# Weight pieces split three ahead, a larger VectorE account and re-spaced gather units in a PEER block on one Trainium2 core

## Chip, core and metric

One core of a Trainium2 chip runs the whole program in one launch. The metric is the device time of that launch in microseconds (us). TensorE (PE) multiplies, VectorE (DVE) and GpSimd (POOL) do elementwise work, ScalarE (ACT) copies and evaluates functions, SyncE (SP) issues transfers. SP, ACT and POOL each work their instructions off in the order in which they stand, and so do PE and DVE.

## What is computed

A decoder block on 512 tokens of width 2048, all in float32: a norm, an input projection, spatial gating and windowed attention, an output projection, and then a mixer that looks experts up by product keys. The mixer is where the time goes:

```python
q = (xf @ w_query).reshape(T, PEER_HEADS, 2, D_QUERY // 2)
s1 = einsum('thd,kd->thk', q[:, :, 0], sub_keys[0])      # 128 keys each
s2 = einsum('thd,kd->thk', q[:, :, 1], sub_keys[1])
v1, i1 = top_k(s1, 16); v2, i2 = top_k(s2, 16)
top_v, flat = top_k(v1[..., :, None] + v2[..., None, :], 16)   # of 256
experts = e1 * 128 + e2                                  # of 16384
gates = softmax(top_v)
u = take(expert_down, experts); a = gelu(einsum('cd,chkd->chk', x, u))
vt = take(expert_up, experts);  out = einsum('chk,chkd->cd', gates * a, vt)
```

The result is x + out, with a last norm. Each token uses 8 x 16 = 128 of the 16384 experts.

## The kernel before

The tokens are divided. For 352 of them (`TD`) the experts are computed densely: every token meets every expert, in 128 blocks of 128 experts, and a gate table that is zero where an expert was not chosen picks the right ones. For the other 160 the chosen rows are gathered from memory.

Dense work. A float32 product is made of three fast matmuls (`mm3`, L164): the weight is split into a rounded part `whi` and a rest `wlo`, the activations likewise. `down(b)` (L1015) makes block b of scores from two weight pieces of 128 x 1024, 48 matmuls of 352 columns. `up(c)` (L1042) takes eight blocks of gated scores through 16 pieces in four quarters q: the first half of a quarter uses two pieces one after the other, the second half two pieces together, 384 matmuls in all. Each of the four column groups m of a quarter is added into `accT` by VectorE at its end (L1092). The order is 88 `down`s, then ten `up`s, then one `down` and an `up`, and then eight (at the end seven) `down`s and an `up` in turn, up to `up(15)`. `make_ga` (L988) multiplies a block of scores by the gate table and splits it on ACT and DVE.

Weight pieces. `Stream` (L117) loads a piece by SP into one of four `wraw` buffers, copies it to `whi` on ACT (L143) and subtracts to `wlo` on DVE or POOL (L145), four buffers each. `get(ahead)` (L150) hands out piece p and has the pieces up to p + ahead split first; ahead is 2 unless a caller says otherwise.

Gathered work runs beside that in "units" (`unit`, L712): POOL issues an indirect transfer of 128 rows of 1024 (L706), and DVE multiplies it into sums with `half_row` (L720, in the down half) or adds it weighted (L732, in the up half). There are 512 units for the first 128 tokens and 128 for the last 32, whose 128 experts lie in four parts of 32 across the partitions. Gather buffers: four `row`, and, once the `late` pool is open (after `down(82)`), four `more`.

The planner. `Pace` (L47) decides while the program is written, at each `mm3`, what VectorE is given next. It keeps an account `vector`: `step` adds 0.98 ns for each ns of matmul, every piece of work is charged to it, and while it is above zero it hands out steps of key selection (`hot`), gate-table steps (`paced`, mostly "quads": four DVE operations L860 that build one-hot rows, then eight small matmuls L873), or a unit, if `gap` ns have passed since the last. `use_pool` (L60) sends a split to DVE when the account is above zero or POOL's own account is below it, and charges 1250; else to POOL, and charges 500. `spread` (L1190) sets `gap` once, at `down(82)`.

The end. `up(15)` also turns finished quarters back into rows (`rows_out`, L1139: 12 transposes into two `dn` buffers, DVE adds, ACT squares, a multiply), finishes the first 128 gathered tokens (`finish_first`, L1153) and the last 32 (`finish_last`, L1166: eight DVE adds of 32 rows fold the four parts), each with `last_norm` (L1119).

## Time and profile before

| | |
|---|---|
| median of three runs | 3058.1 us (3056.44 to 3060.74) |
| the profiled execution, and its span | 3053.1 us, 3051.4 us |
| busy share of the span: PE, weight loads, DVE, ACT, POOL | 94%, 89%, 74%, 38%, 48% |
| moved from and to memory | 779.91 MB, mean 256 GB/s |

The page's time slices and the view of busy time by stage show where each engine is full; the groups of instructions by line, taken in one stage, show what one operation costs there and what ended the idle time before it; the timeline shows single instructions. A mean of a group can hide two prices, and then only the timeline tells them apart. The stages are: key selection and query projection up to 784 us, `down(0)` to `down(79)` up to 1510, the change of pools and `down(80)` to `down(87)` up to 1593, `up(0)` to `up(9)` up to 2288, the alternation up to 2929, and `up(15)` with the end.

### The profile page before, as it was taken

How to read it: one execution, taken by the hardware profiler on the slowest of the kernel's cores; microseconds unless marked ns; L12 is line 12 of the kernel's file. 1: busy time of each engine (PE TensorE's matmuls, PEld its weight loads, DVE VectorE, ACT ScalarE, POOL GpSimd, SP SyncE). 2: the span in 40 equal slices, each digit the busy share in tenths (PEclk: the TensorE clock that was granted, in tenths of full speed). 3: DMA queues.
4: the chain of work that ended last, by engine and by line, in shares of the span. 5: the costliest groups of instructions: out<-in, count | busy, mean ns of one | idle time of the engine just before them, and what ended most of it. 6: DMA issues, size and time to landing. Idle time of an engine off the chain costs nothing. (4 is left out here: it accounts for less than half of the span.)

```text
span 3051.4 us, 44502 instructions
## 1 busy us (share of the span) xinstructions
PE 2867.4 (94%) x16925; PEld 2727.1 (89%) x16925; DVE 2260.2 (74%) x3359; ACT 1152.7 (38%) x1932; POOL 1474.2 (48%) x998
## 2 busy tenths in 40 slices
PE   7999999999999899999989999999999999999976
PEld 6888878799999899999988999998999999999975
DVE  3125642469947999999957888887788889778865
ACT  3244432222333456767824222322232323323223
POOL 2132100123578667777645666666665444344432
PEclk9999999999999999999999999999999999999987
DMA  5221242422379678978798999999989999899983
GB/s 191 86 83 56 76 162 90 146 90 87 122 260 343 215 264 293 317 261 316 264 333 323 357 347 342 337 334 329 353 330 347 334 334 360 315 332 335 347 306 104
DMA packets 265190, 779.91 MB, mean 256 GB/s; under 512 B 25488, under 2 KB 94416, under 8 KB 259408
## 3 DMA queue, kind: packets, MB, share of 16 engines
q1 hardware_dynamic: 151952, 382.75, 36.7%
q0 software_dynamic: 92160, 335.59, 29.0%
q10 hardware_dynamic: 20864, 58.74, 5.0%
q8 instruction: 133, 2.18, 0.3%
q14 instruction: 81, 0.66, 0.1%
HBM read 726.20 MB, written 50.77 MB: 255 GB/s over the span
## 5 line engine op out<-in xcount | busy, mean ns | idle before, releaser
L145 POOL TENSOR_TENSOR wlo<-wraw,whi 128x1024 fp32r<-128x1024 f32 x284 | 701.0, 2477 | 849.1 <-ACT whi L143 813.3
L143 ACT CAST whi<-wraw 128x1024 fp32r<-128x1024 f32 x628 | 641.2, 1048 | 679.3 <-PE up L167 326.8
L168 PE MATMUL up<-gah,wlo 128*128 128x352 f32 x2048 | 673.9, 329 | 47.2 <-POOL wlo L145 44.0
L166 PE MATMUL up<-gah,whi 128*128 128x352 f32 x2048 | 675.2, 330 | 19.9 <-DVE accT L1092 19.2
L145 DVE TENSOR_TENSOR wlo<-wraw,whi 128x1024 fp32r<-128x1024 f32 x344 | 462.1, 1350 | 305.5 <-ACT whi L143 303.8
L166 PE MATMUL dn<-h2d,whi 128*128 128x352 f32 x2048 | 667.3, 326 | 15.2 <-ACT whi L143 15.2
L168 PE MATMUL dn<-h2d,wlo 128*128 128x352 f32 x2048 | 669.7, 327 | 5.8 <-POOL wlo L145 3.6
L167 PE MATMUL up<-gal,whi 128*128 128x352 f32 x2048 | 668.9, 327 | 0.0
L167 PE MATMUL dn<-h2d,whi 128*128 128x352 f32 x2048 | 667.0, 326 | 0.0
L168 PEld LDWEIGHTS up<-gah,wlo 128*128 128x128 f32 x2048 | 394.0, 192 | 56.9 <-POOL wlo L145 53.2
L166 PEld LDWEIGHTS up<-gah,whi 128*128 128x128 f32 x2048 | 394.4, 193 | 27.5 <-DVE accT L1092 18.0
L166 PEld LDWEIGHTS dn<-h2d,whi 128*128 128x128 f32 x2048 | 390.8, 191 | 16.1 <-ACT whi L143 16.1
L168 PEld LDWEIGHTS dn<-h2d,wlo 128*128 128x128 f32 x2048 | 389.5, 190 | 10.3 <-POOL wlo L145 6.9
L167 PEld LDWEIGHTS up<-gal,whi 128*128 128x128 f32 x2048 | 394.7, 193 | 0.0
L167 PEld LDWEIGHTS dn<-h2d,whi 128*128 128x128 f32 x2048 | 389.7, 190 | 0.0
L720 DVE SCALAR_TENSOR_TENSOR row<-row,half_row 128x1024 f32<-128x1024 f32 x236 | 282.6, 1211 | 70.0 <-DMA row<-in_down_rows,idx 55.7
L860 DVE SCALAR_TENSOR_TENSOR p<-iota,eT,gT 128x256 fp32r<-128x256 f32 x352 | 317.0, 959 | 1.9 <-PE tr L873 1.9
L706 POOL DMA_INDIRECT row<-in_down_rows,idx x236 | 249.3, 1056 | 140.5 <-DVE row L720 88.7
L706 POOL DMA_INDIRECT more<-in_up_rows,idx x160 | 184.4, 1152 | 162.0 <-DVE half_row L732 136.3
L706 POOL DMA_INDIRECT row<-in_up_rows,idx x160 | 182.9, 1143 | 145.3 <-DVE half_row L732 115.7
L732 DVE SCALAR_TENSOR_TENSOR half_row<-more,wgt,half_row 128x1024 f32<-128x1024 f32 x160 | 205.1, 1282 | 1.5 <-DMA more<-in_up_rows,idx 0.3
L732 DVE SCALAR_TENSOR_TENSOR half_row<-row,wgt,half_row 128x1024 f32<-128x1024 f32 x156 | 200.0, 1282 | 1.7 <-DMA row<-in_up_rows,idx 0.3
(201 smaller groups left out, 3755.7 us busy)
## 6 DMA issues: line engine op xcount, KB each, us to landing
wraw<-in_down SPq DMA_DIRECT2D x256, 512.0 KB, 5.6
wraw<-in_up SPq DMA_DIRECT2D x256, 512.0 KB, 7.0
wraw<-in_win SPq DMA_DIRECT2D x52, 512.0 KB, 3.8
g_dram<-stage ACTq DMA_DIRECT2D x22, 1024.0 KB, 8.2
g<-g_dram SPq DMA_DIRECT2D x32, 704.0 KB, 9.3
wraw<-in_wout SPq DMA_DIRECT2D x32, 512.0 KB, 3.7
wraw<-in_wq SPq DMA_DIRECT2D x32, 512.0 KB, 3.7
aa<-a_dram SPq DMA_DIRECT2D x88, 176.0 KB, 9.1
```

The source lines that it names most:

```text
L143: self.nc.scalar.copy(hi, src)
L145: eng.tensor_sub(lo, src, hi.bitcast(F32))
L166: nc.tensor.matmul(ps, wh, xh, start=start, stop=False)
L167: nc.tensor.matmul(ps, wh, xl, start=False, stop=False)
L168: nc.tensor.matmul(ps, wl, xh, start=False, stop=stop)
L706: nc.gpsimd.indirect_dma_start(out=t, out_offset=None, in_=src, in_offset=bass.IndirectOffsetOnAxis(ap=idx[i][:, j, h:h + 1], axis=0))
L720: nc.vector.scalar_tensor_tensor(t, t, 1.0, half_row, op0=OP.mult, op1=OP.mult, accum_out=dots[i][:, j, h:h + 1])
L732: nc.vector.scalar_tensor_tensor(half_row, t, wgt[i][:, j:j + 1], half_row, op0=OP.mult, op1=OP.add)
L860: nc.vector.scalar_tensor_tensor(p2[:, j], iota[:, None, :].to_broadcast([P, 2, P]), t[:, 1, k:k + 1], hl[:, k, :, None].to_broadcast([P, ...
```

## The change

- `get(3)` in `down` and in the first halves of `up`: three pieces ahead are split there, with the same four buffers.
- The account grows by 1.12 ns per ns of matmul (0.98 before), and `use_pool` keeps a split on DVE down to an account of -300.
- No unit or step is handed out while column groups 2 and 3 of a second half are written (`pace.held`).
- Units: the gap is 2300 ns up to `down(82)` (2600 before); from then on `spread(at)` sets it anew at each `up`, from the matmul time left less 110 us. The `more` buffers are three.
- In `up(15)`: `rest_of_first` runs at q = 2, not 1. The last 32 tokens are folded by a matmul with a 0/1 matrix `ones`, one 512-column step ahead of each column group of the last quarter, in place of the eight adds. The three row blocks' `last_norm`s stand behind all three blocks' adds and multiplies.
- `FULL`, `used` and the partial table end change nothing here, since 352 = 11 x 32.

```diff
-MORE_ROWS = 4
+MORE_ROWS = 3
...
-        self.gap = 2600.0
+        self.gap = 2300.0
...
     def use_pool(self):
-        if self.vector > 0.0 or self.pool < 0.0:
+        if self.vector > -300.0 or self.pool < 0.0:
...
-        self.vector = max(min(self.vector + 0.98 * ns, 3000.0), -4000.0)
+        self.vector = max(min(self.vector + 1.12 * ns, 3000.0), -4000.0)
...
     def down(b):
-            hi, lo = W.get()
+            hi, lo = W.get(3)
...
             for i in range(2):
-                w = W.get()
+                w = W.get(3)
...
-            if last and q == 1:
+            if last and q == 2:
                 rest_of_first()
-            if last and q == 2:
                 pace.drain()
-                rest_of_last = finish_last()
-            if last and q == 3:
-                rest_of_last()
+                steps_of_last.extend(finish_last())
...
             for m in range(4):
+                pace.held = m > 1
+                if last and q == 3 and steps_of_last:
+                    steps_of_last.pop(0)()
                 for j in range(4, 8):
                     multiply(m, j, w[j // 2 - 2])
...
+            pace.held = False
...
             square(b, n, y, q, nc.vector if q == 3 else nc.gpsimd)
-            if q == 3:
-                last_norm(b, n, y, o_rows[b + 1][:n])
+        if q == 3:
+            for b in range(ND):
+                n = min(P, TD - b * P)
+                last_norm(b, n, late["x"][b], o_rows[b + 1][:n])
...
-                eng = nc.sync if s % 2 else nc.scalar
-                eng.dma_start(t[:n], y_dram[1][s * n:(s + 1) * n, cols])
-                parts.append((t, cols))
-
-        def rest():
-            for t, cols in parts:
-                nc.vector.tensor_add(x[:n, cols], x[:n, cols], t[:n])
-            for q in range(4):
-                square(NB, n, x, q, nc.vector)
-            last_norm(NB, n, x, o_rows[NB - 1][P - n:])
-        return rest
+            t = pg.tile([P, D // 2], F32, name="row", bufs=4)
+            nc.sync.dma_start(t, y_dram[1][:, h * D // 2:(h + 1) * D // 2])
+            parts.append(t)
+        ones = late["fin"].tile([P, EX], F32, name="ones")
+        nc.vector.tensor_reduce(ones, ident.rearrange("p (s m) -> p m s", m=EX), axis=AX.X, op=OP.add)
+
+        def piece(q):
+            cols = slice(q * 512, (q + 1) * 512)
+            ps = ps2.tile([P, 512], F32, name="dn", bufs=2)
+            nc.tensor.matmul(ps[:n], ones, parts[q // 2][:, q % 2 * 512:(q % 2 + 1) * 512],
+                             start=True, stop=True)
+            nc.vector.tensor_add(x[:n, cols], ps[:n], x[:n, cols])
+            square(NB, n, x, q, nc.gpsimd)
+            if q == 3:
+                last_norm(NB, n, x, o_rows[NB - 1][P - n:])
+        return [lambda q=q: piece(q) for q in range(4)]
...
-        pace.gap = (left * TD * COL_NS - 45e3) / len(pace.units)
+            pace.gap = max(2000.0, (left - 110e3) / len(pace.units))
```

What the planner makes of it shows in the order of the instructions. On DVE, in the middle of the 88 `down`s, before (`p` is a quad's one-hot rows, `row` a unit, `oh` and `ef` steps of decoding the keys):

```order
L720 SCALAR_TENSOR_TENSOR row,dots_4083<-row,half_row 128x1024
L860 SCALAR_TENSOR_TENSOR p_11132<-iota,eT,gT 128x256 x4
L720 SCALAR_TENSOR_TENSOR row,dots_4083<-row,half_row 128x1024
L644 TENSOR_TENSOR oh<-dec,iota 128x1024
L649 TENSOR_TENSOR oh<-oh,keyf 128x1024
L651 TENSOR_REDUCE ef<-oh 128x64
L860 SCALAR_TENSOR_TENSOR p_11247<-iota,eT,gT 128x256 x4
L720 SCALAR_TENSOR_TENSOR row,dots_4083<-row,half_row 128x1024
L860 SCALAR_TENSOR_TENSOR p_11295<-iota,eT,gT 128x256 x4
```

and now, on DVE in the same stretch:

```order
L861 SCALAR_TENSOR_TENSOR p_9705<-iota,eT,gT 128x256 x4
L721 SCALAR_TENSOR_TENSOR row,dots_4083<-row,half_row 128x1024
L146 TENSOR_TENSOR wlo<-wraw,whi 128x1024
L721 SCALAR_TENSOR_TENSOR row,dots_4083<-row,half_row 128x1024
L861 SCALAR_TENSOR_TENSOR p_9773<-iota,eT,gT 128x256 x4
L146 TENSOR_TENSOR wlo<-wraw,whi 128x1024
L721 SCALAR_TENSOR_TENSOR row,dots_4083<-row,half_row 128x1024 x2
L861 SCALAR_TENSOR_TENSOR p_9840<-iota,eT,gT 128x256 x4
L721 SCALAR_TENSOR_TENSOR row,dots_4083<-row,half_row 128x1024 x2
```

Units come in pairs, and splits stand on DVE where there were none. On DVE in the stretch of ten `up`s, around a second half, before:

```order
L145 TENSOR_TENSOR wlo<-wraw,whi 128x1024 x2
L732 SCALAR_TENSOR_TENSOR half_row<-more,wgt_4081,half_row 128x1024
L1092 TENSOR_TENSOR accT<-up,accT 128x352
L732 SCALAR_TENSOR_TENSOR half_row<-more,wgt_4081,half_row 128x1024
L1092 TENSOR_TENSOR accT<-up,accT 128x352 x2
L732 SCALAR_TENSOR_TENSOR half_row<-more,wgt_4081,half_row 128x1024
L1092 TENSOR_TENSOR accT<-up,accT 128x352
L145 TENSOR_TENSOR wlo<-wraw,whi 128x1024
```

and now there:

```order
L146 TENSOR_TENSOR wlo<-wraw,whi 128x1024 x2
L733 SCALAR_TENSOR_TENSOR half_row<-row,wgt_4081,half_row 128x1024 x3
L146 TENSOR_TENSOR wlo<-wraw,whi 128x1024
L733 SCALAR_TENSOR_TENSOR half_row<-row,wgt_4081,half_row 128x1024
L146 TENSOR_TENSOR wlo<-wraw,whi 128x1024
L733 SCALAR_TENSOR_TENSOR half_row<-more,wgt_4081,half_row 128x1024
L1099 TENSOR_TENSOR accT<-up,accT 128x352
L733 SCALAR_TENSOR_TENSOR half_row<-more,wgt_4081,half_row 128x1024
L1099 TENSOR_TENSOR accT<-up,accT 128x352 x3
```

No unit stands any more between the last three adds of a quarter, and the split that followed the second half stands ahead of its adds. On DVE in `up(15)`, q = 1 and the start of q = 2, before (`xr` are the dense tokens' rows, `yf` the first gathered tokens):

```order
L145 TENSOR_TENSOR wlo<-wraw,whi 128x1024
L732 SCALAR_TENSOR_TENSOR half_row<-more,wgt_4082,half_row 128x1024
L1160 TENSOR_TENSOR yf<-yf,xf 128x2048
L1122 TENSOR_REDUCE sf<-ss_26853 128x1
L1128 TENSOR_SCALAR yf<-yf,rstd 128x1024
L1148 TENSOR_TENSOR xr_26854<-dn,xr_26854 128x512
L1148 TENSOR_TENSOR xr_26856<-dn,xr_26856 128x512
L1148 TENSOR_TENSOR xr_26858<-dn,xr_26858 96x512
L145 TENSOR_TENSOR wlo<-wraw,whi 128x1024 x2
```

and now:

```order
L146 TENSOR_TENSOR wlo<-wraw,whi 128x1024 x3
L1156 TENSOR_TENSOR xr_26884<-dn,xr_26884 128x512
L1156 TENSOR_TENSOR xr_26886<-dn,xr_26886 128x512
L1156 TENSOR_TENSOR xr_26888<-dn,xr_26888 96x512
L146 TENSOR_TENSOR wlo<-wraw,whi 128x1024
L1099 TENSOR_TENSOR accT<-up,accT 128x352 x4
L146 TENSOR_TENSOR wlo<-wraw,whi 128x1024 x3
L1170 TENSOR_TENSOR yf<-yf,xf 128x2048
L1130 TENSOR_REDUCE sf<-ss_26883 128x1
L1136 TENSOR_SCALAR yf<-yf,rstd 128x1024
```

The gathered tokens' steps stand a quarter later, and no unit is left in this block. Counted over the whole program, splits on DVE go from 344 to 429 and on POOL from 284 to 199; the number of units, 640, stays.

## Rows read from the trace of the kernel before

**Rows 1.** Busy time by stage: stretch, length, PE, PEld, DVE, ACT, POOL, clock, DMA.

```profile
784.00:1057.00 273.00, 257.88 (x1564) 254.27 (x1564) 208.45 (x410) 97.65 (x136) 204.62 (x116) 0.97 0.71 247
1057.00:1510.00 453.00, 445.22 (x2928) 443.56 (x2927) 445.76 (x549) 311.60 (x699) 335.69 (x192) 0.99 0.82 286
1510.00:1593.40 83.40, 72.58 (x451) 70.76 (x450) 50.50 (x79) 34.29 (x70) 36.37 (x26) 0.94 0.89 329
1593.40:2287.60 694.20, 643.96 (x3840) 630.85 (x3841) 564.79 (x717) 208.74 (x261) 429.94 (x301) 0.97 0.91 339
2287.60:2929.10 641.50, 622.43 (x3842) 618.20 (x3841) 542.71 (x619) 200.00 (x245) 288.41 (x242) 0.99 0.93 337
2929.10:3051.40 122.30, 73.81 (x434) 71.65 (x432) 69.61 (x83) 35.95 (x62) 27.24 (x28) 0.80 0.48 175
```

**Rows 2.** The same view of single blocks: eight downs, up(3), up(11).

```profile
2363.80:2425.30 61.50, 61.50 (x387) 61.50 (x386) 52.48 (x53) 21.10 (x30) 24.55 (x22) 1.00 0.90 316
1803.00:1871.50 68.50, 63.64 (x386) 62.56 (x386) 53.62 (x86) 20.15 (x25) 44.04 (x32) 0.98 0.92 342
2425.30:2488.50 63.20, 61.72 (x386) 61.14 (x386) 57.24 (x59) 18.18 (x19) 29.75 (x25) 1.00 0.98 362
```

**Rows 3.** PE by line, 1593 to 2288 us: busy, mean ns, idle before, releasers.

```profile
L168 PE MATMUL up<-gah,wlo 128*128 128x352 f32 x1280 | 423.4, 331 | 39.8 <-POOL wlo L145 39.4
L166 PE MATMUL up<-gah,whi 128*128 128x352 f32 x1280 | 423.2, 331 | 10.8 <-DVE accT L1092 10.1 <-ACT whi L143 0.4 <-ACT accT L1090 0.3
```

**Rows 4.** Waits of the whole run: total us, times, longest us.

```profile
PE up L168 <- POOL wlo L145: 44.0, 25, 3.8
```

**Rows 5.** ACT by line, 1593 to 2288 us.

```profile
L143 ACT CAST whi<-wraw 128x1024 fp32r<-128x1024 f32 x161 | 163.8, 1049 | 233.9 <-PE up L167 146.8 <-DMA wraw<-in_up 46.6 <-POOL wlo L145 38.7
```

**Rows 6.** DVE by line, 1593 to 2288 us.

```profile
L145 DVE TENSOR_TENSOR wlo<-wraw,whi 128x1024 fp32r<-128x1024 f32 x89 | 147.2, 1659 | 37.1 <-ACT whi L143 36.7
...
L1092 DVE TENSOR_TENSOR accT<-up,accT 128x352 f32<-128x352 f32 x143 | 73.2, 518 | 39.1 <-PE up L168 38.8
...
L999 DVE TENSOR_TENSOR gal<-aa,gah 128x352 fp32r<-128x352 f32 x81 | 42.5, 525 | 49.7 <-ACT gah L998 49.7
```

**Rows 7.** DVE by line, 2296 to 2812 us: splits with POOL almost without any.

```profile
L145 DVE TENSOR_TENSOR wlo<-wraw,whi 128x1024 fp32r<-128x1024 f32 x126 | 153.4, 1220 | 31.6 <-ACT whi L143 31.2 <-PE dn L168 0.4
```

**Rows 8.** DVE by line, 1057 to 1510 us.

```profile
L860 DVE SCALAR_TENSOR_TENSOR p<-iota,eT,gT 128x256 fp32r<-128x256 f32 x312 | 287.3, 979 | 1.5 <-PE tr L873 1.5
L720 DVE SCALAR_TENSOR_TENSOR row<-row,half_row 128x1024 f32<-128x1024 f32 x96 | 115.1, 1208 | 4.2 <-DMA row<-in_down_rows,idx 4.1
```

**Rows 9.** POOL by line, 1057 to 1510 us.

```profile
L145 POOL TENSOR_TENSOR wlo<-wraw,whi 128x1024 fp32r<-128x1024 f32 x96 | 240.2, 2504 | 85.2 <-ACT whi L143 84.3
```

**Rows 10.** Timeline of DVE and POOL: start, length, instruction, idle before.

```profile
1230.70 3.81 DVE L860 SCALAR_TENSOR_TENSOR p<-iota,eT,gT 128x256 fp32r<-128x256 f32 x4
...
1277.24 1.67 DVE L860 SCALAR_TENSOR_TENSOR p<-iota,eT,gT 128x256 fp32r<-128x256 f32 x4
...
1231.59 2.63 POOL L145 TENSOR_TENSOR wlo<-wraw,whi 128x1024 fp32r<-128x1024 f32 x1 [1.52 <-ACT whi L143]
```

**Rows 11.** DVE by line, 784 to 1057 us.

```profile
L720 DVE SCALAR_TENSOR_TENSOR row<-row,half_row 128x1024 f32<-128x1024 f32 x51 | 61.2, 1214 | 35.7 <-DMA row<-in_down_rows,idx 35.6
```

**Rows 12.** PE by line in up(15), 2929 us to the end.

```profile
L1145 PE MATMUL dn<-ident,accT 128*128 128x128 f32 (+1 forms) x48 | 7.8, 301 | 25.9 <-DVE xr L1148 25.6 <-DVE accT L1092 0.3
```

**Rows 13.** Timeline of DVE in up(15) and at the end.

```profile
2963.82 2.29 DVE L1160 TENSOR_TENSOR yf<-yf,xf 128x2048 f32<-128x2048 f32 x1 [7.72 <-DMA xf<-x_dram]
...
2972.84 0.75 DVE L1128 TENSOR_SCALAR yf<-yf,rstd 128x1024 f32<-128x1024 f32 x1 [3.51 <-POOL rstd L1126]
...
3004.48 4.95 DVE L1184 TENSOR_TENSOR xf<-xf,more 32x1024 f32<-32x1024 f32 x4
...
3033.47 0.75 DVE L1128 TENSOR_SCALAR xr<-xr,rstd 128x1024 f32<-128x1024 f32 x1 [0.95 <-POOL rstd L1126]
...
3041.54 0.75 DVE L1128 TENSOR_SCALAR xr<-xr,rstd 96x1024 f32<-96x1024 f32 x1 [0.94 <-POOL rstd L1126]
```

More of the change, by code (lines that the diff above doesn't have):

```diff
@@ L40 @@
 TG = 32
-NTG = TD // TG
+NTG = -(-TD // TG)
+FULL = TD // TG
 BIG = 3.0e38
 COL_NS = 0.4505
-MORE_ROWS = 4
+MORE_ROWS = 3
 class Pace:
@@ L882, in products @@
                                                           bufs=4)
+                            used = TD - b * P - 4 * n
+                            if used < TG:
+                                nc.gpsimd.memset(stage[h][:, :, used:], 0.0)
                     o = 4 * (n % 8)
@@ L1171, in finish_last, with spread @@
         for h in range(2):
[L1172 to L1195 removed]
+            t = pg.tile([P, D // 2], F32, name="row", bufs=4)
[13 more added lines that the diff above has]
+        return [lambda q=q: piece(q) for q in range(4)]
+    steps_of_last = []
+    def spread(at):
+        left = sum(48 if k == "d" else 384 for k, i in order[at:]) * TD * COL_NS
+        if pace.units:
+            pace.gap = max(2000.0, (left - 110e3) / len(pace.units))
+    for at, (kind, i) in enumerate(order):
         if kind == "u":
+            spread(at)
             up(i)
```

21 lines of the change are left out of this document (7 added, 14 removed).

## The prediction

> **What bounds the kernel now.** I read the busy time by stage first [rows 1], then single blocks [rows 2], then the groups by line in the stages that lose time, and last the timeline where a group's mean mixes two prices.
>
> PE is the engine to be kept busy. A clean block, eight `down`s with 384 matmuls, takes 61.5 us [rows 2], 0.160 us a matmul. By that rate the ten `up`s (3840 matmuls) need 614 us and take 694: 80 lost. The alternation behind them needs 615 and takes 641.5: 27 lost. `up(15)` needs 61.5 and takes 122 with the end of the program [rows 1]. The reader should see that these three stages, with the change of pools, hold the slack; and that VectorE is nearly full in most of the kernel, at 445.8 of 453 us in the second part of the `down`s.
>
> In the ten `up`s PE waits 39.4 us for a `wlo` from POOL and 10.1 us for `accT`, whose add must free the accumulator [rows 3]; the granted clock is 0.97 there, and 3% of 694 is 21 us of lower clock (1.2 instead of 2.4 GHz, after PE stood still). Together 71 of the 80. The longest wait for POOL is 3.8 us [rows 4]. A `wlo` is late because its piece is (46.6 us of ACT's idle time ahead of `whi` is a transfer of `wraw` [rows 5]), because it takes 2.4 us or more on POOL, and because gathers stand ahead of it in POOL's queue.
>
> In the quads' part of the `down`s VectorE and POOL hold each other up. Four quad operations take 1.67 us alone and 3.81 us when a POOL split of 2.63 us runs among them [rows 10], so the mean of 979 ns [rows 8] is a mixture: 78 quads at 1.67 would be 130 us, they take 287, and the other 157 us belong to 96 POOL splits [rows 9], 1.6 us each.
>
> **The change part by part.** The sum is made against the profiled execution, 3053.1 us (its span is 3051.4, 1.7 lies around it). It is 5.0 under the median, which I add at the end. The numbers of units and splits by stage are counted along the program before and after.
>
> A. `down(0)` to `down(79)`, 784 to 1510 us. 57 units are done here that stood later (147 become 204): 57 x 1.21 = 69 us more for VectorE [rows 8]. 38 splits come from POOL: 38 x 1.22 = 46 us [rows 7]. 31 of them leave the quads' part, at 1.6 us each: 50 us less. Seven key-selection steps go ahead of 784, 16 us by what the code charges for them; VectorE isn't what PE waits for there, and I charge nothing. Balance: +49 us of VectorE time. VectorE is busy 654 of 726 us and idle 72 [rows 1]; 40 of these it waits for gathered rows [rows 8, 11], and I keep that. The other 32 are spots where it was ahead, and I keep 8. So 654 + 49 + 48 = 751: **+25 us**. If a POOL split costs VectorE 2.1 us wherever it meets quads (3.81 - 1.67) and the idle time falls to 25: 654 + 33 + 25 = 712, -14. If the denser units wait more, 85 us idle: +62, which is the upper end.
>
> B. The change of pools, 83.4 us with PE busy 72.6 [rows 1]. A piece is copied ahead of the first `make_ga`s on ACT, not behind them: up to one piece's time, 24 x 0.16 = 3.8 us. **-3** (-9 to +6).
>
> C. The ten `up`s. Per block 4.1 splits leave POOL (7.2 become 3.1), 2.6 units have gone to A (23 become 20.4), 4 more splits stand on DVE. What leaves PE's path: each first-half piece is split 24 matmuls, 3.84 us, sooner, and the longest wait for POOL was 3.8; a split on DVE takes 1.22, not 2.4; no unit delays the last two adds of a quarter, so most of the 10.1 us goes. What is late next is VectorE. Before, it is busy 56.5 us a block and idle 5 more waiting for ACT in `make_ga` (49.7 in all [rows 6]): 61.5, just what PE needs. Now: splits 4 x 1.22 = +4.9; units 2.6 x 1.21 = -3.1; its splits took 1659 ns against 1220 alone [rows 6, 7], 39 us over 72 POOL splits, 0.54 each, so 4.1 x 0.54 = -2.2. Sum -0.4: as full as before. The nearest row is `up(11)`, which took 63.2 us with VectorE busy 57.2 and almost no such waits [rows 2]; `up(3)` with them took 68.5. I take 65.1 a block: **-43 us**. At 63.2 it is -62, at 67.9 (VectorE makes PE wait where POOL did) -15.
>
> D. 2288 to 2929 us. 27 us lost; here nearly all splits are on DVE already, and lead and held units act alone. Two losses come with the change from the first to the last gathered tokens, and come again elsewhere. Half: **-14** (-25 to 0).
>
> E. `up(15)` and the end. PE waits 25.9 us ahead of row transposes [rows 12], twice: at q = 1 while DVE holds at `yf` for a transfer and then for its chain over ACT and POOL, from 2956 to 2973.6, and at q = 3 behind the fold, two groups of 4.95 and the multiplies [rows 13]. The first wait goes, since row blocks no longer stand behind `yf`. The chain itself (2963.8 to 2973.6, 9.8 us [rows 13]) now stands ahead of the next row blocks at q = 2, with two pieces of lead less: I keep 8 us of it. The second wait goes; four short matmuls cost about 2 us, an estimate from the 7.8 us of 48 transposes, and the last 32 tokens' norm, now ahead of the last `accT` add, 1.5. Splits waited 2 to 3 us more, and clock after two stalls 3 us less. -25.9 + 8 + 2 + 1.5 - 6 = **-20** (-27 to -8). The last norms side by side give nothing: the blocks follow each other at 4.04 us (8.07 for two [rows 13]), of which 1.85 is a norm (0.15 + 0.95 + 0.75); DVE still does a norm's sum, waits for POOL and scales before the next, and the three parts only change places. All three output transfers now start within 4 us, which may cost 1.
>
> Sum: 25 - 3 - 43 - 14 - 20 = -55. 3053.1 - 55 = 2998; with the 5.0, **3003 us**.
>
> The Trainium skill ("Perfetto Trace Analysis", Optimizing Scalar/DVE Operations) says that where VectorE is saturated, handing work to another engine, GpSimd too, may help. This change does the opposite in A. By that rule alone the 50 us of relief would not exist. The same section warns that the two share an SBUF read port and so may gain nothing from it, and 3.81 against 1.67 us [rows 10] is on the side of the warning.
>
> **The rivals.**
> 1. VectorE's larger account is hidden in A: the stage ends at its lower bound, -14. Sum -94: 2964. For it: PE itself needs 80 x 48 x 0.16 = 614 us of the 726 there, and the quads' small matmuls. Against: VectorE is at 98% [rows 1]. Chance 0.16.
> 2. VectorE stays the bound in C, -15: the sum is -27, 3031. For it: 61.5 us of work and waits in 61.5. Against: the waits shown are for POOL. Chance 0.18.
> 3. Relief fails: POOL splits delay VectorE as much as before although they are fewer (the lock is met by what is left, and by the new DVE splits). A is then +75: sum -5, 3053. Chance 0.06. This is also what the cited rule would give.
> 4. Slower: **the gather queue in A.** Only four `row` buffers exist there, and units now come in pairs, 204 in the place of 147. Where they stood densest before, VectorE waited 35.6 us over 51 units, 0.70 each [rows 11]; in the quads' part 4.1 over 96 [rows 8]. VectorE works in order, so each such wait holds splits and quads behind it, and PE behind those. At 0.70 for all 204: 143 us in the place of 40, A is 654 + 49 + 143 + 8 - 726 = +128, and the sum +48: 3106. It decides from a mean wait of about 0.47 us a unit, where A eats up the other terms. Against: the quads' part spaced units at 4.7 us and now at some 3.6, nearer to its row than to the other. Chance 0.13.
>
> **How the numbers follow.** The forecast, 2985 to 3022, has 0.47. Rivals 1 and 2 are faster too. Within 0.2% (6 us, about what a measurement of this kernel can tell from no change) I put rival 3's middle and a little of rival 2's upper end; slower is rival 4 and the rest of rival 3. Faster 0.80, same 0.06, slower 0.14. The range leaves out most of rival 4 and the lower half of rival 1: 2964 to 3055.
>
> **What would show it.** Right: the ten `up`s near 651 us with under 15 us of PE waiting for `wlo` and clock near 1.0; the `down` stage near 751 us, VectorE still above 95% busy and quads nearer to 1.67 us; no idle time ahead of L1145's first group in `up(15)`, but one of some 8 us ahead of the second; the last three norms no shorter. Wrong: VectorE idle for rows in A by far more than 40 us (rival 4); PE in the `up`s waiting for DVE as long as it did for POOL (rival 2); a `down` stage no longer than 726 us (rival 1).

## The result and the profile after

The changed kernel takes 3037.9 us (median of 5 runs, 3034.2 to 3043.4), the kernel before, run beside it, 3060.7 (3056.4 to 3064.6). The ratio is 0.9927, with a 95% interval of 0.9911 to 0.9943: faster by 22.8 us, where 55 were forecast. The profiled execution after is 3037.9 us long with a span of 3036.2, right at its median. The profiled execution before, 3053.1, stands 7.6 us under the median of these five runs. The traces thus show 15.2 us between the two spans, and the medians 22.8.

The busy time by stage of the kernel after (stretch, length, PE, PEld, DVE, ACT, POOL, granted clock, DMA share, GB/s); the stages start at the first matmul of `down(0)`, `down(24)`, `down(80)`, `up(0)`, `down(88)` and `up(15)`, so they answer to [rows 1], except that the downs are cut at another place:

```profile
786.70:1000.60 213.90, 193.45 (x1158) 190.35 (x1157) 181.46 (x401) 67.49 (x81) 148.08 (x88) 0.96 0.75 261
1000.60:1576.00 575.40, 540.46 (x3352) 529.88 (x3353) 539.02 (x726) 352.00 (x766) 363.12 (x239) 0.96 0.85 301
1576.00:1651.60 75.60, 69.29 (x434) 68.48 (x433) 45.56 (x76) 30.02 (x58) 33.60 (x24) 0.95 0.87 321
1651.60:2305.90 654.30, 628.36 (x3842) 620.34 (x3842) 548.00 (x676) 208.47 (x261) 303.64 (x235) 0.98 0.92 341
2305.90:2931.20 625.30, 617.35 (x3842) 614.23 (x3842) 521.81 (x607) 205.84 (x250) 249.69 (x209) 1.00 0.90 326
2931.20:3036.20 105.00, 73.74 (x441) 67.98 (x439) 43.52 (x62) 34.20 (x60) 27.00 (x27) 0.88 0.46 162
```

and the same view of the kernel before for the first three and the next seven groups of eight `down`s:

```profile
784.00:977.20 193.20, 188.01 (x1154) 185.41 (x1154) 138.30 (x316) 63.71 (x76) 148.89 (x85) 0.99 0.72 251
977.20:1510.30 533.10, 515.40 (x3339) 512.72 (x3338) 516.20 (x644) 345.70 (x759) 391.42 (x223) 0.98 0.80 279
```

The reader should see that the later stages gave about what was forecast, and that the downs took most of it back. After minus before: the part ahead of the downs +2.7, the downs (A) +20.7 and +42.3, together +63; the change of pools (B) -7.5; the ten ups (C) -39.9; the alternation (D) -16.2; `up(15)` and the end (E) -17.3. In sum -15.

In the downs 3 to 9 the two engines' groups by line say what PE waits for. PE, kernel after, then before (busy, mean ns, idle before, releasers):

```profile
L874 PE MATMUL tr<-p,p 128*128 128x128 f32 x656 | 98.1, 280 | 34.9 <-DVE p L861 34.8
```

```profile
L873 PE MATMUL tr<-p,p 128*128 128x128 f32 x640 | 83.4, 271 | 12.0 <-DVE p L860 10.8 <-ACT whi L143 1.2
L842 PE MATMUL tr<-ident,ef 128*128 128x128 f32 x9 | 2.2, 317 | 5.7 <-DVE ef L651 4.8 <-DVE ef L665 1.0
```

Nearly all of PE's idle time after, 575.4 - 540.5 = 35 us, stands ahead of the quads' products, which wait for VectorE's `p`; before it was 12 and 5.7. PE is also busy longer, 540 us where nearly the same matmuls took 515. The granted clock explains about half of these 25 us: 0.96 in the mean loses 0.04 x 575 = 23 us, 0.98 before lost 0.02 x 533 = 11. Where the rest comes from is open. VectorE is what the stage waits for. Its groups in the same stretch, after:

```profile
L861 DVE SCALAR_TENSOR_TENSOR p<-iota,eT,gT 128x256 fp32r<-128x256 f32 x332 | 271.7, 877 | 0.0
L721 DVE SCALAR_TENSOR_TENSOR row<-row,half_row 128x1024 f32<-128x1024 f32 x158 | 188.1, 1212 | 30.4 <-DMA row<-in_down_rows,idx 29.0 <-ACT half_row L720 1.1
L146 DVE TENSOR_TENSOR wlo<-wraw,whi 128x1024 fp32r<-128x1024 f32 x32 | 40.6, 1269 | 4.4 <-ACT whi L144 4.4
L645 DVE TENSOR_TENSOR oh<-dec,iota 128x1024 bf16<-128x1024 f32 x8 | 19.6, 2449 | 0.0
...
L652 DVE TENSOR_REDUCE ef<-oh 128x64 f32<-128x1024 bf16 x8 | 9.8, 1220 | 0.3
```

and before:

```profile
L860 DVE SCALAR_TENSOR_TENSOR p<-iota,eT,gT 128x256 fp32r<-128x256 f32 x331 | 304.3, 977 | 1.5 <-PE tr L873 1.5
L720 DVE SCALAR_TENSOR_TENSOR row<-row,half_row 128x1024 f32<-128x1024 f32 x111 | 133.1, 1209 | 12.8 <-DMA row<-in_down_rows,idx 12.6
```

The units and the new splits bring 55 and 41 us; the quads give back 33. POOL still makes 81 splits there (112 before):

```profile
L146 POOL TENSOR_TENSOR wlo<-wraw,whi 128x1024 fp32r<-128x1024 f32 x81 | 196.9, 2431 | 49.0 <-ACT whi L144 47.8
```

In the first three groups of downs VectorE waits less for rows than before (27.3 us there):

```profile
L721 DVE SCALAR_TENSOR_TENSOR row<-row,half_row 128x1024 f32<-128x1024 f32 x46 | 54.9, 1213 | 18.3 <-DMA row<-in_down_rows,idx 13.4 <-ACT asp L1040 4.8
```

In the ten ups PE's wait for POOL's `wlo`, 39.4 us [rows 3], is gone, and its wait for `accT` has grown from 10.1 to 17.9:

```profile
L167 PE MATMUL up<-gah,whi 128*128 128x352 f32 x1280 | 418.6, 327 | 23.9 <-DVE accT L1099 17.9 <-ACT whi L144 4.8 <-ACT accT L1097 1.3
...
L169 PE MATMUL up<-gah,wlo 128*128 128x352 f32 x1280 | 415.7, 325 | 2.0 <-DVE wlo L146 1.2 <-POOL wlo L146 0.7
```

In `up(15)` 25.9 us ahead of the row transposes [rows 12] have become 11.8. By the timeline of PE, 8.18 of them are a single wait at the start of the second group, the chain of the gathered tokens:

```profile
L1153 PE MATMUL dn<-ident,accT 128*128 128x128 f32 (+1 forms) x48 | 7.4, 289 | 11.8 <-DVE xr L1156 9.2 <-DVE accT L1099 2.6
```

```profile
2980.52 1.09 PE L1153 MATMUL dn<-ident,accT 128*96 128x128 f32 x4 [8.18 <-DVE xr L1156]
```

### The profile page after: what moved, and what is told of

It reads as the page before. It is cut to its first block, busy times and chain, and to the rows that moved or that the text cites. A ratio compares the mean times of both kernels' runs of the same rounds, so it can differ in the third digit from the quotient of the medians.

```text
span 3036.2 us, 44558 instructions
## 1 busy us (share of the span) xinstructions
PE 2875.5 (95%) x16933; PEld 2729.3 (90%) x16933; DVE 2256.4 (74%) x3437; ACT 1162.6 (38%) x1932; POOL 1276.6 (42%) x917
## 4 chain that ended last, share of the span: by engine, by line
PE 60%; DVE 18%; DMA 10%; issue 5%; POOL 3%; ACT 2%; SPq 0%; ACTq 0%; POOLq 0%; DVEq 0%
PE up L167 7%; PE up L169 7%; PE up L168 7%; PE acc L167 7%; PE acc L169 7%; PE acc L168 7%; PE dn L168 5%; PE dn L167 5%; PE dn L169 5%; DVE p L861 4%; DMA wraw<-in_up 4%; DVE row L721 4%; DMA row<-in_down_rows,idx 3%; DVE wlo L146 2%; DMA row<-in_up_rows,idx 2%
## 5 line engine op out<-in xcount | busy, mean ns | idle before, releaser
L146 POOL TENSOR_TENSOR wlo<-wraw,whi 128x1024 fp32r<-128x1024 f32 x199 | 492.1, 2479 | 850.9 <-ACT whi L144 815.7
L146 DVE TENSOR_TENSOR wlo<-wraw,whi 128x1024 fp32r<-128x1024 f32 x429 | 528.1, 1242 | 294.1 <-ACT whi L144 293.9
L707 POOL DMA_INDIRECT row<-in_down_rows,idx x275 | 297.8, 1083 | 304.7 <-DVE row L721 243.3
L721 DVE SCALAR_TENSOR_TENSOR row<-row,half_row 128x1024 f32<-128x1024 f32 x275 | 328.0, 1213 | 75.1 <-DMA row<-in_down_rows,idx 60.1
L707 POOL DMA_INDIRECT row<-in_up_rows,idx x182 | 210.2, 1155 | 174.6 <-DVE half_row L733 152.2
L861 DVE SCALAR_TENSOR_TENSOR p<-iota,eT,gT 128x256 fp32r<-128x256 f32 x352 | 279.7, 854 | 0.0
L733 DVE SCALAR_TENSOR_TENSOR half_row<-row,wgt,half_row 128x1024 f32<-128x1024 f32 x181 | 232.5, 1284 | 5.2 <-DMA row<-in_up_rows,idx 2.9
L707 POOL DMA_INDIRECT more<-in_up_rows,idx x138 | 160.2, 1161 | 118.4 <-DVE half_row L733 90.0
L1005 ACT CAST gah<-aa 128x352 fp32r<-128x352 f32 x128 | 62.3, 487 | 310.7 <-DVE aa L1001 272.2
## 6 DMA issues: line engine op xcount, KB each, us to landing
g_dram<-stage ACTq DMA_DIRECT2D x22, 1024.0 KB, 10.1
```

The costliest lines, as they stand in the source:

```text
L146: eng.tensor_sub(lo, src, hi.bitcast(F32))
L707: nc.gpsimd.indirect_dma_start(out=t, out_offset=None, in_=src, in_offset=bass.IndirectOffsetOnAxis(ap=idx[i][:, j, h:h + 1], axis=0))
L721: nc.vector.scalar_tensor_tensor(t, t, 1.0, half_row, op0=OP.mult, op1=OP.mult, accum_out=dots[i][:, j, h:h + 1])
L733: nc.vector.scalar_tensor_tensor(half_row, t, wgt[i][:, j:j + 1], half_row, op0=OP.mult, op1=OP.add)
L861: nc.vector.scalar_tensor_tensor(p2[:, j], iota[:, None, :].to_broadcast([P, 2, P]), t[:, 1, k:k + 1], hl[:, k, :, None].to_broadcast([P, ...
L1005: nc.scalar.copy(hi, t)
```

## The experiments

Three groups, each on one chip beside runs of the kernel before. The times by stage in the tables are cut at the same matmuls as above.

### Lead and account, each alone

The first kernel is the one before with only the lead of three:

```
-            hi, lo = W.get()
+            hi, lo = W.get(3)
...
-                w = W.get()
+                w = W.get(3)
```

> The kernel before with three pieces ahead alone (in down and in up's first halves); account, gap and the end as before. Theory 1 (the lead of 3.84 us is what frees the ten ups, the account is what lengthens the downs): downs 0 to 79 stay at 726 us (within 6), the ten ups fall from 694 to 655 to 665, the last block stays at 122, total 30 to 40 us under the kernel before. Theory 2 (the gain in the ups comes from splits moved to VectorE and from units moved out of them): the ups stay above 680, total within 15 us of before.

Measured: 3070.6 us, ratio 1.0025 (0.9996 to 1.0055): no gain. PE in the ten ups:

```profile
L166 PE MATMUL up<-gah,whi 128*128 128x352 f32 x1280 | 426.8, 333 | 31.3 <-DVE accT L1092 26.1 <-ACT whi L143 4.5 <-issue 0.6
...
L168 PE MATMUL up<-gah,wlo 128*128 128x352 f32 x1280 | 421.9, 330 | 17.4 <-POOL wlo L145 17.2 <-DVE wlo L145 0.2
```

The earlier split does shorten the wait for POOL, from 39.4 to 17.2 us, but the wait for `accT` grows from 10.1 to 26.1, and the ups take 697 us where they took 694. One wait took the place of the other. So the second theory's marks hold, but neither theory had the downs right: both left them at 726 us, and they take 195.7 + 568.3 = 764. It is the downs 3 to 9 that grew, with a quad operation at 1089 ns beside 113 POOL splits:

```profile
980.30:1548.60 568.30, 529.45 (x3346) 520.07 (x3345) 552.91 (x648) 351.65 (x763) 385.83 (x226) 0.97 0.76 265
```

```profile
L860 DVE SCALAR_TENSOR_TENSOR p<-iota,eT,gT 128x256 fp32r<-128x256 f32 x332 | 342.2, 1089 | 0.0
```

The second kernel has only the new account:

```
-        self.gap = 2600.0
+        self.gap = 2300.0
...
-        if self.vector > 0.0 or self.pool < 0.0:
+        if self.vector > -300.0 or self.pool < 0.0:
...
-        self.vector = max(min(self.vector + 0.98 * ns, 3000.0), -4000.0)
+        self.vector = max(min(self.vector + 1.12 * ns, 3000.0), -4000.0)
```

> The kernel before with the account alone (1.12, -300, gap 2300 up to down 82); two pieces ahead, units in up spaced by one gap set at down 82. Theory 1: downs 0 to 79 lengthen from 726 to about 789 us as in the changed kernel, the ups gain 10 to 20 (POOL makes 3 splits a block, not 7), total 30 to 50 us slower than before. Theory 2: the ups fall to 655 or less and the total is within 25 us of the kernel before or under it. If two pieces ahead make PE stall more, the downs exceed 800.

Measured: 3052.1 us, ratio 0.9956 (0.9926 to 0.9985). Downs 3 to 9 and the ups:

```profile
1003.50:1582.10 578.60, 536.85 (x3352) 524.20 (x3353) 542.77 (x726) 349.03 (x766) 365.90 (x239) 0.97 0.84 299
...
1661.90:2314.80 652.90, 630.44 (x3841) 619.15 (x3840) 560.94 (x672) 209.20 (x261) 325.93 (x236) 0.98 0.91 338
```

The account alone makes the ups as short as in the changed kernel (654.3), as the second theory had it, with two pieces of lead and nothing held back, and makes the downs as long. Both the gain in C and the loss in A belong to it.

### The account in one part, and quads without POOL

The changed kernel with the account of before up to the change of pools:

```
-        self.gap = 2300.0
+        self.gap = 2600.0
+        self.rate, self.floor = 0.98, 0.0
...
             open_late()
+            pace.rate, pace.floor = 1.12, -300.0
             spread(at)
```

> The changed kernel with the account of before (0.98, 0, gap 2600) up to down 82 and its own from there. The downs then do 147 units as before, so the ups get 23 a block. Theory 1: downs 0 to 79 back to 726 us (within 8), that is 63 less than in the changed kernel; the ups give back part: 660 to 672 in the place of 654; the rest as in the changed kernel; total 40 to 55 us under the changed kernel. Rival (three pieces ahead is what lengthens the downs, by binding ACT and VectorE to PE's progress): downs stay above 770, total within 10 us of the changed kernel.

Measured: 3088.6 us, ratio 1.0077 (1.0040 to 1.0114). Neither expectation held: all downs take 763 us, between the 726 of the one and the 770 of the other, and the whole is 51 us over the changed kernel. The downs 3 to 9 still take 568 us (with the lead of three, as in the first kernel), and the ups 698. In the ups 23 units a block are left, as before the change, and only 3 to 4 splits a block are on POOL: PE hardly waits for POOL there, but long for `accT`.

```profile
PE up L168 <- DVE accT L1100: 37.6, 21, 5.2
...
PE up L170 <- POOL wlo L147: 2.6, 2, 1.7
```

So to take the splits from POOL without moving units out of the ups brought nothing here. This and the first kernel say that lead and account in the ups are not enough.

Now the suspicion in A: that POOL's splits hold up the quads. The changed kernel, with every split on VectorE while quads are pending:

```
-        if self.vector > -300.0 or self.pool < 0.0:
+        if self.vector > -300.0 or self.pool < 0.0 or 0 < len(self.paced) < 104:
```

> The changed kernel with every split on VectorE while quads are made (about downs 22 to 80), none on POOL. The account then hands out 158 units in downs 0 to 79, not 204. Lock theory (a POOL split costs VectorE 1.6 us where it meets quads, more than the 1.22 us of the split itself): a quad falls from 3.3 us on average to 1.67, VectorE's work in downs 24 to 79 from 78 to about 68 us per eight downs, PE becomes the bound: downs 0 to 79 fall from 789 to 725 to 745; ups 660 to 670; total 35 to 60 us under the changed kernel. Rival (VectorE is simply full, a split handed to it costs its 1.22 us): 80 more splits are 98 us less 46 units at 1.2, downs 0 to 79 at 810 to 840, total 20 to 60 us over the changed kernel.

Measured: 3018.7 us, ratio 0.9862 (0.9808 to 0.9917), 19 us under the changed kernel (in another group of runs), though VectorE has 81 more splits in the downs 3 to 9. Some 35 to 60 were expected. The downs, 721 us in all, went by the lock theory (725 to 745), the ups (660 to 670) did not. The downs 3 to 9, and the ups:

```profile
999.60:1505.70 506.10, 506.10 (x3343) 506.06 (x3344) 426.86 (x716) 349.35 (x759) 131.48 (x112) 0.99 0.83 293
...
1578.70:2267.80 689.10, 639.76 (x3842) 629.68 (x3841) 571.21 (x750) 209.59 (x262) 331.89 (x260) 0.97 0.92 343
```

```profile
L861 DVE SCALAR_TENSOR_TENSOR p<-iota,eT,gT 128x256 fp32r<-128x256 f32 x332 | 138.7, 480 | 0.0
```

A quad operation takes 480 ns in the mean, 877 in the changed kernel. PE is busy all of the time: 506 us is its own time there. VectorE's busy time falls from 539 to 427 us, though part of that is work that went elsewhere: the splits, charged to the account, leave 46 fewer units in this stage; the ups have 23 units a block again and take 689 us.

### Quads without POOL, and the units kept

To take the two apart, a split in the quads' part is charged at 700 instead of 1250, which gives the same number of units to each stage as the changed kernel has:

```
-        if self.vector > -300.0 or self.pool < 0.0:
-            self.vector -= 1250.0
+        quads = 0 < len(self.paced) < 104
+        if self.vector > -300.0 or self.pool < 0.0 or quads:
+            self.vector -= 700.0 if quads else 1250.0
```

> The changed kernel, with every split on VectorE while quads are pending (as in the run with quads without GpSimd), and such a split charged 700 ns to the account in place of 1250, so that the planner sets the same 156 units into the downs 3 to 9 as the changed kernel does (the earlier run had 110 there) and 20 to 21 into each up block. Theory 'lock': the downs lose their time to GpSimd splits that hold up the quads' VectorE operations, and the units as such fit beside TensorE: downs 3 to 9 take 506 to 525 us (575 in the changed kernel), quads 0.48 us each, the ten ups 650 to 660 as in the changed kernel, in all some 2965 to 2990 us. Rival 'VectorE time': 46 more units at 1.28 us add 59 us of VectorE work to the 427 us of the earlier run, and with them the downs go to 550 us or more; in all 3010 or more. Rival 'DMA in the downs': 24 MB more in the downs 3 to 9 would need 340 GB/s there; if transfers then wait, the idle time is in front of wlo and whi, and the stretch takes 530 to 550.

Measured: 2974.3 us, ratio 0.9716 (0.9666 to 0.9766): faster than both kernels. Downs 3 to 9, ups, alternation, and VectorE's groups in the first of these:

```profile
999.60:1515.60 516.00, 512.68 (x3351) 509.88 (x3352) 478.49 (x813) 351.94 (x771) 193.98 (x158) 0.99 0.92 336
...
1586.70:2241.10 654.40, 627.78 (x3842) 620.31 (x3841) 549.15 (x679) 209.32 (x262) 303.21 (x235) 0.98 0.92 341
2241.10:2864.10 623.00, 616.96 (x3842) 614.38 (x3841) 520.42 (x605) 204.36 (x248) 249.09 (x209) 1.00 0.90 326
```

```profile
L722 DVE SCALAR_TENSOR_TENSOR row<-row,half_row 128x1024 f32<-128x1024 f32 x158 | 189.4, 1214 | 20.1 <-DMA row<-in_down_rows,idx 20.1
L862 DVE SCALAR_TENSOR_TENSOR p<-iota,eT,gT 128x256 fp32r<-128x256 f32 x338 | 141.2, 479 | 0.0
L147 DVE TENSOR_TENSOR wlo<-wraw,whi 128x1024 fp32r<-128x1024 f32 x113 | 137.6, 1219 | 15.9 <-ACT whi L145 15.8
...
L653 DVE TENSOR_REDUCE ef<-oh 128x64 f32<-128x1024 bf16 x8 | 9.8, 1220 | 0.3
L646 DVE TENSOR_TENSOR oh<-dec,iota 128x1024 bf16<-128x1024 f32 x8 | 9.8, 1219 | 0.0
```

The same 158 units that are said to cost the stage 55 us now stand beside PE: 516 us instead of 575. 81 splits on POOL cost more than 81 x 1.22 = 99 us of splits on VectorE. All other stages are within 5 us of the changed kernel's, and 64 us are gained (between two groups of runs).

The same with the account of before in the first three groups of downs, once with 500 and once with 700 as the charge:

```
-        self.vector = max(min(self.vector + 1.12 * ns, 3000.0), -4000.0)
+        rate = 0.98 if len(self.paced) >= 104 else 1.12
+        self.vector = max(min(self.vector + rate * ns, 3000.0), -4000.0)
```

(with the limit of -300 set to 0 there too).

> As the run with the same units and no GpSimd splits, but the account of before (0.98 for a nanosecond, limit 0) for the first three down blocks, and a charge of 500 ns in the quads' part so that some 17 more units go there. Theory 'account at the start': the 20 us that the first three downs gained in the changed kernel (193 to 214 us) come from the larger account alone, which brings splits and units among the choices' VectorE work: the first three downs fall back to 194 to 197 us, and the whole to some 15 to 20 us less than the run it is built on, unless the extra units cost downs 3 to 9 more than 5 us. Rival 'order of the choices': the 20 us come from steps that the ahead of three moves; then the first three downs stay at 212 to 216.

> As the run with the same units and no GpSimd splits (2974 us), with the account of before for the first three down blocks and the charge of 700 ns kept. First three downs 197 to 201 us in place of 215; downs 3 to 9, into which the quads that the small account puts off now fall, with 11 GpSimd splits at their start: 520 to 535 in place of 516 (540 in the run with 500 ns, which set 17 more units there); ups 655 to 668, since some 7 units more are left. If the first stage's gain is kept by the others: 2960 to 2970 us; if work that is put off is only paid later: 2974 to 2985.

Measured: 2985.4 us, ratio 0.9755 (0.9703 to 0.9807), and 2975.7 us, ratio 0.9687 (0.9654 to 0.9720). The first three groups fall to 199.7 and 199.0 us (215.5), so 16 of the 20 us that they had grown are the account's. But the next stage takes 539.9 and 523.4 (516.0), and the alternation 630 and 633 (623). In the second kernel 16 us are gained, and the stages behind pay back 19 in sum: work that is put off is paid later. The second kernel's expectation of 520 to 535 held. The first kernel's did not: it was to be 15 to 20 us faster than the run that it is built on, with 5 us at most for the extra units, and is 11 slower.

### What bounds the ups

The kernels up to here move 338 to 343 GB/s in the ups, at a DMA share of 0.91 to 0.92. That looked like a limit, with the units' bytes as its cause. Two kernels on the base of the one before, which keep the order: half of each gather, and half of each unit's VectorE work.

```
+            c = D // 4 if "p" in late else D // 2
+            short[fetched] = c < D // 2
             nc.gpsimd.indirect_dma_start(
-                out=t, out_offset=None, in_=src,
+                out=t[:, :c], out_offset=None,
+                in_=src.rearrange("r (a c) -> (r a) c", c=c),
...
+            if short[u]:
+                x = t[:, None, :D // 4].to_broadcast([P, 2, D // 4])
+                z = half_row.rearrange("p (a c) -> p a c", a=2)
...
-                    nc.vector.scalar_tensor_tensor(half_row, t, wgt[i][:, j:j + 1], half_row,
+                    nc.vector.scalar_tensor_tensor(z, x, wgt[i][:, j:j + 1], z,
...
```

> The kernel before, from the first up block's opening on each gather fetches 2 KB for a partition in place of 4 KB (half of each row, of other places of the table), and VectorE works over 1024 elements as before by reading the half row twice. So half of the gathered values are left out of the sums. Nothing else moves in the order. Theory 'bytes': the ups run at what the DMA engines deliver, 338 to 343 GB/s in five kernels; ten ups move 235 MB, of which 60 MB are then gone, and they fall from 694 us to TensorE's 620 to 640 us, the alternation from 641 to 618 to 628, and the whole by 70 to 95 us. Rival 'VectorE time': the ups are bound by VectorE's units and splits and the waits behind them; then the ups stay at 680 to 700.

```
+            c = D // 4 if "p" in late else D // 2
...
-                nc.vector.scalar_tensor_tensor(t, t, 1.0, half_row, op0=OP.mult, op1=OP.mult,
+                nc.vector.scalar_tensor_tensor(t[:, :c], t[:, :c], 1.0, half_row[:, :c], op0=OP.mult, op1=OP.mult,
...
-                    nc.vector.scalar_tensor_tensor(half_row, t, wgt[i][:, j:j + 1], half_row,
+                    nc.vector.scalar_tensor_tensor(half_row[:, :c], t[:, :c], wgt[i][:, j:j + 1], half_row[:, :c],
```

> The kernel before, from the first up block's opening on each unit's VectorE operation works over 512 of the 1024 gathered elements, and the gathers stay whole. So half of the gathered values are left out of the sums. VectorE is relieved of some 23 times 0.55 us in an up block, 12 to 14 us of 56. Theory 'bytes': the ups stay within 8 us of 694, the whole within 15 us of before. Rival 'VectorE time': the ups fall by 60 us or more, as they would if VectorE's work set their end.

Measured, the ups with half the gathers, then with half the VectorE work:

```profile
1602.70:2292.10 689.40, 639.12 (x3841) 626.53 (x3842) 564.51 (x717) 206.73 (x261) 438.08 (x301) 0.97 0.75 253
```

```profile
1592.90:2271.50 678.60, 636.42 (x3841) 627.88 (x3840) 452.86 (x715) 207.59 (x260) 427.42 (x302) 0.97 0.93 346
```

Half the bytes: 253 GB/s in the place of 339, and 689.4 us for 694.2. The bytes theory falls. Half of VectorE's work: its busy time falls by 112 us and the stage by only 15.6. That is neither within the 8 us of the bytes theory nor the rival's 60: PE's wait for POOL stays where it was, and only the one for `accT` goes (10.1 to 3.2 us):

```profile
L168 PE MATMUL up<-gah,wlo 128*128 128x352 f32 x1280 | 422.0, 330 | 38.3 <-POOL wlo L145 38.3
...
L166 PE MATMUL up<-gah,whi 128*128 128x352 f32 x1280 | 420.1, 328 | 3.9 <-DVE accT L1093 3.2 <-ACT whi L143 0.6
```

The whole took 3035.6 (ratio 0.9904, 0.9872 to 0.9935) and 3038.0 us (0.9932, 0.9904 to 0.9959).

The last corner: units moved out of the ups, but the account of before in the ups.

```
-        self.gap = 2600.0
+        self.gap = 2300.0
+        self.rate, self.floor = 1.12, -300.0
...
             open_late()
+            pace.rate, pace.floor = 0.98, 0.0
```

> The kernel before with the new account (1.12, limit -300, gap 2300) up to the first up block, and with the account of before (0.98, limit 0) from there on. Pieces are split two ahead, nothing is held back. The downs then leave some 20.4 units for an up block, as in the changed kernel, but 5 to 6 splits of a block stay on GpSimd (3 in the changed kernel, 8 before). Theory 'units': the ups are set by VectorE and GpSimd together, and what shortens them is that 2.6 units a block have gone to the downs, whatever the lead, the account or the hold in the ups are: ten ups 650 to 665 us, TensorE's waits 20 to 30 us in them. Rival 'account in the ups': the splits that the larger account takes from GpSimd are what shortens them; then waits for GpSimd's wlo come back, and the ups stay at 675 to 695. Downs 3 to 9 in either case 570 to 580 and the whole 3045 to 3060 (units) or 3070 to 3090 (account).

Measured: 3087.2 us, ratio 1.0066 (1.0039 to 1.0093). The ups, and PE in them:

```profile
1657.90:2338.00 680.10, 638.59 (x3843) 626.36 (x3842) 539.68 (x651) 208.37 (x261) 361.39 (x253) 0.97 0.88 324
```

```profile
L169 PE MATMUL up<-gah,wlo 128*128 128x352 f32 x1280 | 419.9, 328 | 26.5 <-POOL wlo L146 24.5 <-DVE wlo L146 1.9
```

The rival's marks hold (ups of 675 to 695 us, the whole 3070 to 3090, the wait for POOL back at 24.5); yet 14 us of the 40 are gained, so the units alone do something too. With the kernels above, the time of the ten ups in four corners:

| | units left in the ups (23 a block) | units moved out (20 to 21) |
|---|---|---|
| account of before | 694 (before), 697 (lead of three) | 680 |
| new account | 689, 698 | 654 (after), 645 to 665 in six others |

With 23 units the new account only exchanges the wait for POOL for one for VectorE. With 20 units the old account still leaves late POOL splits. Only the two together gave the 40 us.

### The account and the quads alone, and the last norms

The kernel before with the new account and the quads' rule only: no lead, no hold, no re-spacing, the old end.

```
-        self.gap = 2600.0
+        self.gap = 2300.0
...
+        quads = 0 < len(self.paced) < 104
+        if self.vector > -300.0 or self.pool < 0.0 or quads:
+            self.vector -= 700.0 if quads else 1250.0
...
-        self.vector = max(min(self.vector + 0.98 * ns, 3000.0), -4000.0)
+        self.vector = max(min(self.vector + 1.12 * ns, 3000.0), -4000.0)
```

> The kernel before with only the larger account (1.12, limit -300, gap 2300) and with every split on VectorE while quads are pending, charged 700 ns there. Pieces are split two ahead, nothing is held back, no re-spacing at each up block, the last steps as before. Theory 'units and lock': lead, hold and re-spacing bring nothing; downs 3 to 9 take 510 to 530 us, the ten ups 650 to 660, the alternation 620 to 630, and only the end is longer than in the run with the same units and no GpSimd splits (113 in place of 105): 2980 to 2990 us. Rival 'the lead is needed once the downs are relieved': with two ahead PE waits for wlo in the downs or the ups, and the whole takes 3000 us or more.

Measured: 3004.2 us, ratio 0.9780 (0.9747 to 0.9814). By its time that is in the rival's range, 3000 or more, but the waits for `wlo` that the rival names are not there: PE idles 2 us in the downs 3 to 9 and waits 6 for POOL's `wlo` in the ups.

```profile
1002.40:1512.80 510.40, 508.63 (x3344) 506.38 (x3344) 479.24 (x813) 345.22 (x763) 200.76 (x160) 1.00 0.93 340
1594.40:2259.10 664.70, 633.32 (x3842) 620.77 (x3841) 563.83 (x671) 208.46 (x261) 318.41 (x232) 0.98 0.90 331
2883.70:2997.50 113.80, 73.93 (x434) 71.66 (x432) 62.59 (x77) 35.86 (x62) 20.95 (x23) 0.83 0.46 162
```

Against the run with all of the change and the same rule, the downs 3 to 9 are 6 us shorter, the ups 10 longer, the change of pools 10 longer (81.6 against 71.1) and the end 9 longer; of these, 6 and 10 are no more than identical code showed from trace to trace. The lead is worth something at the change of pools: 71 to 77 us in the eight kernels that have it, 80 to 83 in five of the six that don't (75 in the sixth).

The changed kernel with the last norms as before:

```
-        if q == 3:
-            for b in range(ND):
-                n = min(P, TD - b * P)
-                last_norm(b, n, late["x"][b], o_rows[b + 1][:n])
+            if q == 3:
+                last_norm(b, n, y, o_rows[b + 1][:n])
```

> The changed kernel with the last norms written as before, each behind its own row block. Theory 'nothing from it': the last stage ends with the last row block's chain either way, the stage of up 15 and the end stays at 105 us within 1.5, and the whole within 4 us of the changed kernel's 3038. Rival 'side by side': the three norms overlap, and without that the stage takes 109 us or more.

Measured: 3030.3 us, ratio 0.9858 (0.9823 to 0.9892). The last stage:

```profile
2925.10:3030.30 105.20, 73.73 (x442) 67.98 (x440) 43.48 (x62) 34.32 (x60) 26.99 (x27) 0.88 0.45 162
```

105.2 against 105.0 us: the norms side by side give nothing. The whole was expected within 4 us of 3038 and is 7.6 under it, in another group of runs; in the trace this lies in the ups (645 against 654), whose instructions are the same in both.

## Why the prediction was half right

The sum said -55; the traces show -15. By its terms, against the profiled execution:

- **A, +25, measured +63: the step that failed.** That is at the upper end that was given, +62, though not for the reason that was given for it. The number of units (57) and of splits (38) was right, and 57 x 1.21 + 38 x 1.22 = 115 us of new work came: in the downs 3 to 9 alone 55 and 41 by the rows above. Two terms were mis-sized.
  - The relief, 31 splits x 1.6 = 50 us. The quads gave back 33 in the downs 3 to 9, where nearly all of them stand, or 1.05 us for each split taken away: the mean of 1.6 us for each POOL split was taken for the price of those that go. With 479 ns as a quad operation's own time, a split cost before (977 - 479) x 331 / 112 = 1.47 us, after (877 - 479) x 332 / 81 = 1.63. Their number alone doesn't set that price: with the lead alone, 113 splits cost (1089 - 479) x 332 / 113 = 1.79. And the 33 is uncertain: in the trace with half the gathers, whose code up to the change of pools is that of before, the quads took 320.3 us (line below), and against that they gave back 49. The remedy was too weak as well: without POOL the whole excess goes.
  - The idle time. VectorE was to wait 48 us, 24 less than before, and was idle for 789.3 - 181.5 - 539.0 = 69, as before (72). The waits for rows came as kept, 13.4 + 29.0 = 42 us where 40 were put. But of the other 32 us, "spots where it was ahead", of which 8 were kept, 26 stayed; 12 of these are waits of the new splits for ACT's `whi`, 7.8 and 4.4 us, of which there were none before. This miss is the firmer one: in the three traces of the code before VectorE idles 69 to 74 us in the downs, in the changed kernel and the one with the norms inside 69 and 66.
  - In sum VectorE is busy 66 us more (forecast 49), idle 3 less (forecast 24): the 38 us that are missing.
- **B, -3, measured -7.5**, inside its bounds. The lead brings it.
- **C, -43, measured -40. The size was right, the reason was not, so the hit is in part luck.** That "each first-half piece is split 24 matmuls, 3.84 us, sooner" does nothing by itself: the kernel with the lead alone keeps 697 us. Nor are the held units needed: the account alone reaches 653. What frees the ups is that 2.6 units a block (2.3 by the traces, 230 to 207 in the ten ups) have gone to the downs, and that at the same time fewer splits are on POOL. What the prediction weighed up on VectorE (splits +4.9 us a block, units -3.1, shorter splits -2.2) was the heart of it; the lead and the hold show no part in it. It follows that the gain in C takes units that A has to do, and that rival 2 (VectorE the bound in C) is what happens when the units stay: 689 to 698 us.
- **D, -14, measured -16**, but by the account (626 us with it alone), where the prediction named the lead and the held units (635 with the lead alone).
- **E, -20, measured -17**, as written: the first wait gone, one of 8.18 us ahead of the second group where 8 were kept. Half of it comes with the new account in the downs: with that and the old end the stage takes 113.6, 112.3 and 113.8 us in three kernels.
- Last norms: nothing, as forecast.

Of the rivals, the third ("relief fails", A +75) is the nearest in A; C to E then kept the sum below 3053. Rival 2's total, 3031, comes nearer to 3038, but by chance: its cause, ups that gain only 15 us, did not come. The gather queue did not decide: VectorE waited 42 us for rows over the 204 units, 0.21 each, where 0.47 was the turning point.

On the rule of the Trainium skill ("Perfetto Trace Analysis", Optimizing Scalar/DVE Operations) that was weighed there: the trace is on the side of the warning. In the downs 3 to 9, handing splits to POOL where VectorE was full cost VectorE more than doing them itself. The Trainium skill ("SBUF — State Buffer", Who interferes with whom) says that a VectorE operation with two inputs in SBUF contends with a GpSimd one that reads SBUF, and that a reduce, or one with a single SBUF input outside the two-port modes, does not. The rows agree in each case. `p` 877 to 479 ns and `oh<-dec,iota` 2449 to 1219 without POOL's splits; the units, whose second input `half_row` is in PSUM, 1212 and 1214; the TENSOR_REDUCE 1220 in both.

What stays open: why the lead of three makes the downs 3 to 9 longer under the account of before (568 us in both such kernels, a quad operation at 1089 ns). The same code of before took 533, 533 and 549 there in three traces, so some of it may be chance meetings of splits and quads, but not all. And the four corners of the ups say which two things are needed together, not by which chain of waits. Why a POOL split costs the quads 1.47 us in one kernel and 1.79 in another is open too; two traces of the same code gave 1.47 and, by this line of the kernel with half the gathers, (1026 - 479) x 331 / 113 = 1.60:

```profile
L872 DVE SCALAR_TENSOR_TENSOR p<-iota,eT,gT 128x256 fp32r<-128x256 f32 x331 | 320.3, 1026 | 1.5 <-PE tr L885 1.5
```

## What to carry to other kernels

Before work is handed to POOL to relieve VectorE, look for the two prices of VectorE's own operations beside it: where a short two-input operation has one price alone and twice that with POOL running, the hand-over is paid for by VectorE. Don't count on a mean price for each piece taken away: here it was 1.47, 1.60 and 1.79 us at nearly the same number of pieces, and taking a part of them away gave back 33 us where 50 were forecast (49 against another trace); with all of them gone the excess was gone. Where a planner moves work from one stage to another, set the account up over both stages: here the units that left the ups for the 40 us went to downs that had no room for them and grew by 42, and the whole gain came only when the downs had been given room.

## What the runs showed of the hardware

- 81 POOL splits of 2.43 us cost VectorE 132 us in the quads (877 instead of 479 ns, 332 times), and with them PE 35 us of waits and a busy time 28 to 34 us longer: 540 us at a granted clock of 0.96, 513 and 506 at 0.99, for nearly the same matmuls. The clock explains some 18 of these (0.04 x 575 = 23 us lost against 0.01 x 516 = 5); the rest is open.
- A DMA share of 0.91 at 339 GB/s was no limit in the ups: halving the gathers' bytes gave 253 GB/s and the same time within 5 us. In the downs 3 to 9 PE was busy for 512.7 of 516.0 us at 336 GB/s. The Trainium skill ("SBUF — State Buffer", A bandwidth-pool intuition that's wrong (but worth ruling out)) gives some 358 GB/s for HBM and a core and calls HBM, not SBUF, almost always the bottleneck; in these ups the row is against it.
- The ups of identical code differed by 9 us between two traces (645 and 654), and the downs 3 to 9 by 16. A stage's difference of that size between two single traces says nothing about a change.
